# The low parts of the mixer's and the branches' weights on VectorE instead of GpSimd

## The chip, the core and the metric

The kernel runs on one core of a Trainium2 chip. The core has five engines that each work through a queue of their own in order: TensorE (PE in the profile: matmuls, with their weight loads as PEld), VectorE (DVE), ScalarE (ACT), GpSimd (POOL) and SyncE (SP), which here issues most of the loads. The metric is the device time of one execution in microseconds (us), the median over runs. Lower is better.

## The reference, cut to what matters

One layer of a streaming encoder, for 512 tokens of 1024 features in float32:

```python
h = modulate(rmsnorm(x, norm1_g), sh1, sc1)          # sh, sc, gt: columns of silu(c) @ w_ada + b_ada
qa, ka, va, qkb, vb, ob, ib, fb, ga, gb = split(h @ w_in)
y_a = chunk_band_attention(qa, ka, va, rel_bias)     # mixer A, 8 heads x 64
y_b = sigmoid(ob) * rmsnorm(mlstm(silu(conv(qkb)), vb, ib, fb))   # mixer B, 4 heads x 128
y = sigmoid(ga) * (y_a @ w_branch_a) + sigmoid(gb) * (y_b @ w_branch_b)
x = x + gt1 * (y @ w_out)
h2 = modulate(rmsnorm(x, norm2_g), sh2, sc2)
x = x + gt2 * peer_ffn(h2, w_peer_q, peer_sub_keys, peer_u, peer_v)   # 8 heads, best 16 of 128 x 128 experts
out = rmsnorm(x, final_g)
```

## The kernel before

Each large float32 product is made of three matmuls in the type float32r. Both operands are split into a high part (the value rounded to float32r) and a low part (the value minus the high part), and `mm3` (L162 to L165) adds high x high, high x low and low x high in one PSUM bank.

Weights come in pieces of 128 partitions x 1024 numbers, 512 KB each. `load` (L133) lets SP issue the transfer into one of four buffers (`wst`). `split` (L142) then cuts a piece into two halves of 512 columns. For each half ACT copies the high part (`whi`, L150), and one engine subtracts to make the low part (`wlo`, L153). Five buffers of each kind exist. Which engine subtracts is read from a list, `lanes["now"]`, in turn (L151). The list changes with the stage: one list for the start (L897), `LANES_A` (L53) from there to the end of the branches, `LANES_F` for the scores and `LANES_V` for the last stage. The loads of the conditioning weights `w_ada` use the same four `wst` buffers; their dot products are DVE's, at L178.

The stages in order are:

- the start (`start`, L266): the first norm, 16 conditioning columns and the values of both mixers (8 pieces);
- mixer A (`mixer_a`, L317: keys, queries, masked softmax in `ps_s`, `sb` and `mx`) and mixer B (`mixer_b`, L374: gate rows from L389, convolutions in `conv`, L439, head norm from L510), interleaved with each other, with the later conditioning columns (`ada_late`) and with the branch gates (`gates`, L531);
- the branches (`branches`, L545), the output projection and the second norm;
- scores, selection and experts, which take the larger part of the time and start at about 482 us.

The program text gives the order in which work may start, but not the order of each queue: the tile framework plans that from estimated times when the program is built (`schedule_with_timeline_sim=True` in the last lines of the kernel). When the costs or engines of some instructions change, the queues are planned anew.

Of the kernel before, what the change touches and what calls it, by code (L numbers as in the profile page):

```python
# [19 lines left out]
DRAM = bass.MemoryType.DRAM  # L20
# [17 lines left out]
HOLD = 8  # L38
# [4 lines left out]
E1 = 40  # L43
# [8 lines left out]

LANES_A = lambda nc: [nc.gpsimd]  # L53
LANES_F = lambda nc: [nc.vector, nc.gpsimd, nc.gpsimd]
# [6 lines left out]
def weave(*gens):  # L61
    """One generator that steps several in turn; each is (generator, steps per round)."""
    live = [list(g) for g in gens]
    while live:
        for g in list(live):
            for _ in range(g[1]):
                try:
                    next(g[0])
                except StopIteration:
                    live.remove(g)  # L70
                    break
        yield
# [8 lines left out]
def tile_block(  # L81
# [19 lines left out]
    nc = tc.nc  # L101
# [40 lines left out]
    def split(t, pool=None, bufs=WB):  # L142
        """float32 -> two float32r parts whose sum is the value, in two halves."""
        pool = pool or wpool
        parts = []
        for i in range(2):
            cs = slice(i * HW, (i + 1) * HW)
            hi = pool.tile([P, HW], F32R, tag="whi", name="whi", bufs=bufs)
            lo = pool.tile([P, HW], F32R, tag="wlo", name="wlo", bufs=bufs)
            nc.scalar.copy(hi, t[:, cs])  # L150
            e = lanes["now"][rot[0] % len(lanes["now"])]  # L151
            rot[0] += 1
            e.tensor_tensor(out=lo, in0=t[:, cs], in1=hi.bitcast(F32), op=ALU.subtract)  # L153
            parts.append((hi, lo))
        return parts

    def cut(w, a, n):
        """Columns a .. a + n of a split piece."""
        i, o = divmod(a, HW)
        return tuple(x[:, o : o + n] for x in w[i])  # L160
# [10 lines left out]

# [1 line left out]

    def ada(cols):
        """Columns of silu(c) @ w_ada + b_ada."""
        for j in cols:
            t = load(w_ada[j])
            nc.vector.scalar_tensor_tensor(  # L178
                junk(), t, 0.5, state["srow"], op0=ALU.mult, op1=ALU.mult, accum_out=mod[:, j : j + 1]
            )  # L180
        j0, n, step = cols[0], len(cols), cols[1] - cols[0]
        js = slice(j0, j0 + (n - 1) * step + 1, step)
        nc.vector.tensor_add(mod[:, js], mod[:, js], cst[:, C_BADA + js.start : C_BADA + js.stop : step])
# [23 lines left out]
    def rstd_rows(squares):  # L207
        """1 / rms of every token, the same in all partitions, from the squares of blocks of features."""
        ps = bank("w", "ps_ss")
        for i in range(4):  # L210
            for k, sq in enumerate(squares):
                nc.tensor.matmul(
                    ps[:, i : i + 1], sq[:, i * P : (i + 1) * P], ones[:, :1], start=k == 0, stop=k == len(squares) - 1
                )
        rs = spool.tile([P, 4], F32, tag="rs4", name="rs4")
        nc.scalar.activation(rs, ps[:, :4], AF.Sqrt, scale=1.0 / D, bias=epst)
        nc.vector.reciprocal(rs, rs)
        ps = bank("w", "ps_rs")
        for i in range(4):
            nc.tensor.matmul(  # L220
                ps[:, i * P : (i + 1) * P], rs[:, i : i + 1].broadcast_to([P, P]), ident, start=True, stop=True
            )
        return ps

    def norm_block(hT, k, t, rbc, gs, sh0):
        """Modulated RMSNorm of one block of 128 features, split in two parts."""
        h = state["fp"].tile([P, S], F32, tag="hf", name="hf", bufs=3)
        nc.vector.tensor_mul(h, t, rbc)
        nc.scalar.activation(h, h, AF.Identity, scale=gs[:, k : k + 1], bias=mod[:, sh0 + k : sh0 + k + 1])
        nc.scalar.copy(hT[0][:, k, :], h)  # L230
        nc.vector.tensor_sub(hT[1][:, k, :], h, hT[0][:, k, :].bitcast(F32))
        return h
# [4 lines left out]
    pieces = {}  # L237
# [9 lines left out]
    def proj_t(ps, w, hT):  # L247
        """[128 features, tokens]: one piece of 8 x 128 weights."""
        for k in range(KD):
            mm3(ps, cut(w, k * P, P), (hT[0][:, k, :], hT[1][:, k, :]), k == 0, k == KD - 1)  # L250

    def proj_n(ps, nm, j, hT):
        """[tokens, 512 features] for the four token tiles: one of four pieces of 2 x 512 weights."""
        w = piece(nm, j)
        for kk in range(2):
            k = 2 * j + kk
            for i in range(4):
                mm3(
                    ps[i],
                    (hT[0][:, k, i * P : (i + 1) * P], hT[1][:, k, i * P : (i + 1) * P]),  # L260
                    cut(w, kk * 512, 512),
                    k == 0,
                    k == KD - 1,
                )

    def start(ap, bp):  # L266
        """First norm, with the values of both mixers as its blocks come in."""
        hT = features("hT")
# [46 lines left out]

# [1 line left out]
    def mixer_a(ap, hT, va, y_hi, y_lo):  # L317
        """Chunked band attention, heads in pairs."""
        kaT = ap.tile([P, 4, S], F32, name="kaT", bufs=1)
# [54 lines left out]
    def mixer_b(bp, hT, vb, y_hi, y_lo):  # L374
        """mLSTM in its quadratic form, stabilised per row."""
        kbT = bp.tile([P, BH, S], F32, name="kbT", bufs=1)

        # rows of the gates: log input gate, log forget gate, prefix sums per token tile
        wgs = [bp.tile([P, KD, 32 + BH], F32R, name=f"wgs{i}", bufs=1) for i in range(2)]
# [151 lines left out]
    def gates(tp, hT):  # L531
        """tanh(g / 2) of the branch gates, 128 features of both branches at a time."""
        for f in range(KD):
# [11 lines left out]
    def branches(gp, gate, y_hi, y_lo):  # L545
        """Gated sum of the branches, output projection, residual; x2 goes to DRAM."""
        z_hi = gp.tile([P, KD, S], F32R, name="z_hi", bufs=1)
# [57 lines left out]

# [1 line left out]
    def scores(cp, h2T):  # L607
        """Slots (row, column, gate) of the 16 best experts of every token and head."""
        slots = state["slots"]
# [35 lines left out]
    def top16(vals, places, data):  # L645
        """The 16 largest of each row, in order, and where they stand; data is spoilt."""
        nc.vector.max(vals[:, :8], data)
# [5 lines left out]
    def select(cp, h, sv, i16, best, slots):  # L653
        """A head's best 16 sums of one row and one column score, for all tokens."""
        idx = cp.tile([P, 4, 2, TOPK], F32, tag="idx", name="idx")
# [40 lines left out]
    def gathered(cp, i):  # L696
        """A token tile from gathered rows: gelu(u_e . h2) of its slots, then the weighted rows of v."""
        slots = state["slots"][:, i]
# [36 lines left out]
    def build(cp, i, slots):  # L735
        """Gate of every expert for 128 tokens, [column, row, token] blocks, kept in DRAM."""
        ps = bank("g", "ps_slT")
# [36 lines left out]

# [1 line left out]
    def gather_side(cp):  # L776
# [8 lines left out]
    def hidden(e, h2T, tag, g):  # L785
        """gelu(u_e . h2) of 128 experts for the dense token tiles."""
        u = split(load(u_t[e]))
# [4 lines left out]
    def ahead(up, h2T, held):  # L792
        """Hidden values of the first E1 blocks of experts: HOLD of them stay, the others go to DRAM."""
        for e in range(E1):
# [10 lines left out]
    def output(cp, vp, h2T, held):  # L805
        """Sum over all experts of weight x row of v for the dense token tiles."""
        nt = 4 - NG
# [48 lines left out]
    def finish(cp, i, halves):  # L856
        """Residual and final norm of a token tile."""
        if "rows" not in state:
# [25 lines left out]
    def step(g, n):  # L884
        """Steps a generator n times; false when it has ended."""
        return all(next(g, 0) is None for _ in range(n))


    with pool("ypool", 1) as yp, pool("fpool") as fp, ExitStack() as tstack:
# [5 lines left out]
        with pool("bpool") as bp:  # L895
            with pool("apool", side="right") as ap:
                lanes["now"] = [nc.gpsimd, nc.vector]  # L897
                hT, va, vb = start(ap, bp)
# [20 lines left out]
    def paced(main, side, rate):  # L919
        """Steps the side work `rate` times for each step of the main work."""  # L920
        due = 0.0
# [36 lines left out]
def layout(inputs):  # L958
    """The inputs in the order in which the kernel reads them; nothing but copies."""
    f = {k: np.ascontiguousarray(v) for k, v in inputs.items()}  # L960
# [67 lines left out]
```

## Time and profile before

| | |
|---|---|
| runs of the kernel before | 1803.69, 1800.38, 1801.46 us; median 1801.46 |
| span of the profiled execution | 1804.3 us |
| PE, DVE, ACT, POOL busy | 96%, 75%, 47%, 54% of the span |
| start / mixers and gates / branches and output projection | 0 to 62 / 62 to 383 / 383 to 482 us |

The profile records one execution. "Busy" is the time in which an engine executes; waiting and issuing of transfers don't count. A wait is put down to the instruction that ended last before it. In the chain of waits one goes back from the last instruction to what released it, and so on, so an entry there is time on the path that set the end. "issue" in it is time for which the profile shows no reason. [...]

### The profile page before, as it was taken

What the parts mean: (1) busy time and instruction counts of PE and PEld (TensorE: products, weight loads), DVE (VectorE), ACT (ScalarE), POOL (GpSimd) and SP (SyncE); (2) the same over time, 40 slices, a digit from 0 to 9 for tenths busy, and PEclk for the clock granted to TensorE, in tenths of its full rate; (3) what the DMA queues carried; (4) which work ended last, traced back from release to release, by engine and by line L of the source; (5) the groups of instructions that cost most, each with busy time, mean ns of one, the idle gap of its engine ahead of it and who ended that gap; (6) DMA issues with size and microseconds to landing.
All of it is one profiled execution on the core that took longest, in us unless ns stands there. A gap on an engine that the chain in (4) does not pass through costs nothing.

```text
span 1804.3 us, 25525 instructions
## 1 busy us (share of the span) xinstructions
PE 1726.0 (96%) x8671; PEld 1493.6 (83%) x8671; DVE 1353.3 (75%) x2756; ACT 839.1 (47%) x1624; POOL 974.1 (54%) x804
## 2 busy tenths in 40 slices
PE   5999999999999987999989999999999999999997
PEld 4766678878798787888989999999999999998886
DVE  7357655565579998877458888989988998998445
ACT  4534545433543334999734434333443343434443
POOL 1322224444257676887546656766767766673221
PEclk9989999999999998999999999999999999999999
DMA  8423224463232233455798999889999989988552
GB/s 283 151 70 107 95 81 150 164 234 105 107 110 92 88 109 138 190 204 205 266 390 316 326 339 346 324 326 360 324 342 347 349 321 351 346 283 305 209 205 105
DMA packets 129940, 413.35 MB, mean 229 GB/s; under 512 B 12049, under 2 KB 38801, under 8 KB 128274
## 3 DMA queue, kind: packets, MB, share of 16 engines
q1 hardware_dynamic: 91218, 252.33, 39.8%
q0 software_dynamic: 38592, 159.40, 23.4%
q8 instruction: 68, 1.11, 0.2%
q14 instruction: 62, 0.51, 0.1%
HBM read 376.03 MB, written 35.66 MB: 228 GB/s over the span
## 4 chain that ended last, share of the span: by engine, by line
PE 75%; DVE 12%; ACT 6%; DMA 4%; issue 1%; POOL 1%; SPq 0%; DVEq 0%; ACTq 0%; POOLq 0%
PE acc L163 10%; PE acc L165 10%; PE acc L164 10%; PE ps_act L164 8%; PE ps_act L165 8%; PE ps_act L163 8%; ACT gst L767 3%; DMA wst<-in_w_ada 2%; DVE wlo L153 2%; DVE junk L178 1%; PE ps_s L341 1%; PE ps_g L766 1%; ACT oa L761 1%; PE ps_ya L361 1%; PE ps_pq L163 1%
## 5 line engine op out<-in xcount | busy, mean ns | idle before, releaser
L153 POOL TENSOR_TENSOR wlo<-wst,whi 128x512 fp32r<-128x512 f32 x245 | 335.6, 1375 | 374.1 <-ACT whi L150 330.9
L150 ACT CAST whi<-wst 128x512 fp32r<-128x512 f32 x408 | 252.3, 622 | 475.9 <-PE ps_act L164 282.6
L165 PE MATMUL ps_act<-h2T_hi,wlo 128*128 128x384 f32 x1024 | 348.4, 340 | 5.7 <-DVE wlo L153 4.6
L163 PE MATMUL ps_act<-h2T_hi,whi 128*128 128x384 f32 x1024 | 347.4, 339 | 0.0
L164 PE MATMUL ps_act<-h2T_lo,whi 128*128 128x384 f32 x1024 | 347.2, 339 | 0.0
L164 PE MATMUL acc<-wlo,ehi 128*128 128x512 f32 x768 | 299.1, 391 | 0.0
L163 PE MATMUL acc<-whi,ehi 128*128 128x512 f32 x768 | 293.9, 391 | 4.6 <-ACT whi L150 4.6
L165 PE MATMUL acc<-whi,elo 128*128 128x512 f32 x768 | 286.9, 391 | 0.0
L150 ACT CAST whi<-vst 128x512 fp32r<-128x512 f32 x256 | 158.0, 620 | 181.6 <-PE acc L165 144.2
L710 POOL DMA_INDIRECT ur<-in_u_r,ei x128 | 153.7, 1201 | 116.1 <-DVE junk L713 96.0
L153 POOL TENSOR_TENSOR wlo<-vst,whi 128x512 fp32r<-128x512 f32 x85 | 131.7, 1549 | 152.2 <-ACT whi L150 137.1
L724 POOL DMA_INDIRECT vr<-in_v_r,ei x128 | 163.7, 1279 | 89.7 <-DVE sum_v L730 70.4
L165 PEld LDWEIGHTS ps_act<-h2T_hi,wlo 128*128 128x128 f32 x1024 | 194.0, 189 | 8.1 <-DVE wlo L153 5.9
L163 PEld LDWEIGHTS ps_act<-h2T_hi,whi 128*128 128x128 f32 x1024 | 194.3, 190 | 3.7
L164 PEld LDWEIGHTS ps_act<-h2T_lo,whi 128*128 128x128 f32 x1024 | 194.2, 190 | 3.7
L730 DVE SCALAR_TENSOR_TENSOR sum_v<-vr,act,sum_v 128x1024 f32<-128x1024 f32 x127 | 181.2, 1427 | 1.4 <-DMA vr<-in_v_r,ei 0.7
L153 DVE TENSOR_TENSOR wlo<-wst,whi 128x512 fp32r<-128x512 f32 x163 | 132.9, 817 | 60.0 <-ACT whi L150 59.7
L163 PEld LDWEIGHTS acc<-whi,ehi 128*128 128x128 f32 x768 | 144.9, 189 | 33.1 <-ACT whi L150 5.0
L713 DVE SCALAR_TENSOR_TENSOR junk<-ur,h 128x1024 bf16<-128x1024 f32 x128 | 171.0, 1336 | 0.9
L165 PEld LDWEIGHTS acc<-whi,elo 128*128 128x128 f32 x768 | 144.0, 188 | 30.6 <-DVE elo L841 0.4
L164 PEld LDWEIGHTS acc<-wlo,ehi 128*128 128x128 f32 x768 | 144.3, 188 | 28.4
L153 DVE TENSOR_TENSOR wlo<-vst,whi 128x512 fp32r<-128x512 f32 x171 | 132.5, 776 | 28.7 <-ACT whi L150 28.6
(300 smaller groups left out, 3081.0 us busy)
## 6 DMA issues: line engine op xcount, KB each, us to landing
wst<-in_u_t SPq DMA_DIRECT2D x128, 512.0 KB, 5.8
vst<-in_v_e SPq DMA_DIRECT2D x128, 512.0 KB, 6.1
wst<-in_w_pieces SPq DMA_DIRECT2D x76, 512.0 KB, 3.4
wst<-in_w_ada SPq DMA_DIRECT2D x48, 512.0 KB, 4.0
gd<-gst POOLq DMA_DIRECT2D x12, 2048.0 KB, 7.4
gq<-gd SPq DMA_DIRECT2D x16, 1536.0 KB, 15.1
ad<-gelu SPq DMA_DIRECT2D x8, 768.0 KB, 5.5
aq<-ad SPq DMA_DIRECT2D x8, 768.0 KB, 6.0
```

The source lines that it names most:

```text
L150: nc.scalar.copy(hi, t[:, cs])
L153: e.tensor_tensor(out=lo, in0=t[:, cs], in1=hi.bitcast(F32), op=ALU.subtract)
L163: nc.tensor.matmul(o, a[0], b[0], start=first, stop=False)
L164: nc.tensor.matmul(o, a[0], b[1], start=False, stop=False)
L165: return nc.tensor.matmul(o, a[1], b[0], start=False, stop=last)
L178: nc.vector.scalar_tensor_tensor(junk(), t, 0.5, state["srow"], op0=ALU.mult, op1=ALU.mult, accum_out=mod[:, j : j + 1])
L341: nc.tensor.matmul(pss[:, :n], qaT[po : po + 64, cs], kaT[po : po + 64, hp, :n], start=True, stop=True)
L710: nc.gpsimd.indirect_dma_start(out=t, out_offset=None, in_=u_r, in_offset=bass.IndirectOffsetOnAxis(ap=ei[:, j : j + 1], axis=0))
L713: nc.vector.scalar_tensor_tensor(junk(), t, 1.0, state["h2"][i], op0=ALU.mult, op1=ALU.mult, accum_out=act[:, j : j + 1])
L724: nc.gpsimd.indirect_dma_start(out=t, out_offset=None, in_=v_r, in_offset=bass.IndirectOffsetOnAxis(ap=ei[:, j : j + 1], axis=0))
L730: nc.vector.scalar_tensor_tensor(sum_v, t, act[:, j : j + 1], sum_v, op0=ALU.mult, op1=ALU.add)
L767: nc.scalar.copy(st[:, :, t4 * 4 : t4 * 4 + 4].rearrange("p i t -> p t i"), ps.rearrange("p (t i) -> p t i", t=4),)
```

## The change

Two lists of engines are changed. In the start the low parts were made on GpSimd and VectorE by turns and are now all made on VectorE. From there to the end of the branches they were all made on GpSimd and are now all made on VectorE. The lists of the later stages stay. The other lines of the diff take docstrings and comments away and leave the line numbers as they are.

```diff
-LANES_A = lambda nc: [nc.gpsimd]
+LANES_A = lambda nc: [nc.vector]
 LANES_F = lambda nc: [nc.vector, nc.gpsimd, nc.gpsimd]
 LANES_V = lambda nc: [nc.vector, nc.vector, nc.gpsimd]
...
             with pool("apool", side="right") as ap:
-                lanes["now"] = [nc.gpsimd, nc.vector]
+                lanes["now"] = [nc.vector]
                 hT, va, vb = start(ap, bp)
                 lanes["now"] = LANES_A(nc)
```

## Rows read from the trace of the kernel before

**Rows 1.** The page's first part: busy us of each engine, its share of the span, and the number of instructions.

```profile
PE 1726.0 (96%) x8671; PEld 1493.6 (83%) x8671; DVE 1353.3 (75%) x2756; ACT 839.1 (47%) x1624; POOL 974.1 (54%) x804
```

**Rows 2.** Busy time by stage: the stretch in us, its length, the busy us of each engine with the number of instructions, the granted clock of PE, the busy share of the DMA engines and GB/s. The last row sums five stretches from 0 to 482 us.

```profile
105.00:236.00 131.00, 125.06 (x561) 85.87 (x559) 80.86 (x246) 60.88 (x157) 30.57 (x24) 0.93 0.27 89
236.00:383.00 147.00, 143.13 (x651) 112.77 (x650) 80.88 (x166) 66.43 (x156) 55.29 (x44) 0.98 0.46 155
383.00:482.00 99.00, 96.75 (x446) 80.18 (x444) 49.41 (x61) 35.89 (x61) 42.02 (x33) 0.98 0.39 138
sum 482.00, PE 447.92 PEld 343.28 DVE 273.25 ACT 212.63 POOL 158.49; mean PE 89.58 PEld 68.66 DVE 54.65 ACT 42.53 POOL 31.70
```

**Rows 3.** Busy time, columns as in rows 2: PE, PEld, DVE, ACT, POOL, in the score stage.

```profile
540.00:700.00 160.00, 141.55 (x730) 126.23 (x728) 159.42 (x696) 54.13 (x97) 110.83 (x111) 0.97 0.29 100
```

**Rows 4.** What PE waited for from 62 to 482 us: who waited, what for, us in total, times, longest. The longest waits on DVE; further down the list there is no low part of a weight piece (`wlo`).

```profile
PE ps_hbT L524 <- DVE hb L517: 3.9, 1, 3.9
PE ps_s L341 <- DVE mx L346: 2.7, 2, 2.2
...
PE ps_col L429 <- DVE grow L421: 1.7, 1, 1.7
```

**Rows 5.** The chain of waits in the start: start us, us, what.

```profile
21.45 1.62 DVE wlo L153
...
23.91 0.91 issue
...
33.28 1.37 DVE wlo L153
...
49.99 1.58 issue
...
59.55 1.30 POOL wlo L153
```

**Rows 6.** The instructions that write `wlo` from `wst`, over the whole span: how many, shortest, median and longest duration in ns, first and last start in us.

```profile
L153 POOL TENSOR_TENSOR wlo<-wst,whi x245: 1263/1295/2281, 21.0 to 1606.1; 128x512 fp32r<-128x512 f32 x123
...
L153 DVE TENSOR_TENSOR wlo<-wst,whi x163: 664/686/2704, 21.4 to 1598.4; 128x512 fp32r<-128x512 f32 x163
```

**Rows 7.** In the branches: one low part of GpSimd and the DVE instructions beside it from the timeline (start us, us, engine, line, operation), and L559 from the groups of 383 to 482 us (busy us, mean ns of one).

```profile
400.59 1.29 POOL L153 TENSOR_TENSOR wlo<-wst,whi 128x512 fp32r<-128x512 f32 x1 [1.06 <-ACT whi L150]
...
400.07 0.69 DVE L558 SCALAR_TENSOR_TENSOR gb<-gb,ps_br 128x512 f32<-128x512 f32 x1 [1.11 <-PE ps_br L165]
400.80 1.63 DVE L559 TENSOR_TENSOR ga<-ga,gb 128x512 f32<-128x512 f32 x1
...
L559 DVE TENSOR_TENSOR ga<-ga,gb 128x512 f32<-128x512 f32 x8 | 13.0, 1625 | 0.3
```

**Rows 8.** The gate rows of mixer B on DVE: the shortest, median and longest scan in ns, and the scans and the subtraction behind them in the timeline.

```profile
L402 DVE TENSOR_TENSOR_SCAN arow<-ones,mall x4: 386/900/1436, 88.5 to 91.5; 4x128 f32<-4x128 f32 x4
...
88.46 3.41 DVE L402 TENSOR_TENSOR_SCAN arow<-ones,mall 4x128 f32<-4x128 f32 x4
...
91.91 1.58 DVE L403 TENSOR_TENSOR rr<-rr,arow 4x512 f32<-4x512 f32 x1
```

**Rows 9.** Busy time by stretch, columns as in rows 2 (the engines are PE, PEld, DVE, ACT, POOL in that order).

```profile
82.00:94.00 12.00, 10.30 (x47) 8.21 (x46) 6.22 (x13) 8.98 (x12) 5.29 (x4) 1.00 0.15 46
150.00:176.00 26.00, 22.24 (x112) 16.60 (x111) 21.68 (x44) 9.80 (x22) 9.65 (x6) 0.96 0.41 135
323.00:378.00 55.00, 51.13 (x231) 41.13 (x230) 32.00 (x66) 19.15 (x47) 19.78 (x15) 0.98 0.59 201
```

**Rows 10.** DVE's timeline among the convolutions.

```profile
152.00 0.43 DVE L459 TENSOR_SCALAR kbT<-cv 128x512 f32<-128x512 f32 x1
...
157.87 0.74 DVE L451 SCALAR_TENSOR_TENSOR cv<-raw,cst,cv 128x512 f32<-128x512 f32 x1
...
161.00 1.70 DVE L451 SCALAR_TENSOR_TENSOR cv<-raw,cst,cv 128x512 f32<-128x512 f32 x1
...
164.47 1.40 DVE L459 TENSOR_SCALAR kbT<-cv 128x512 f32<-128x512 f32 x1
...
166.36 2.44 DVE L451 SCALAR_TENSOR_TENSOR cv<-raw,cst,cv 128x512 f32<-128x512 f32 x2
...
172.09 1.37 DVE L459 TENSOR_SCALAR kbT<-cv 128x512 f32<-128x512 f32 x1
```

**Rows 11.** The chain of waits ahead of the last head norm.

```profile
330.96 2.20 DVE junk L178 x2
...
336.73 1.23 DVE junk L178 x2
...
338.49 1.72 DVE cv L451
...
343.99 1.63 POOL wlo L153 x2
...
353.44 2.26 DVE junk L178 x2
...
367.09 1.07 issue
```

**Rows 12.** Waits as in rows 4: DVE's from 62 to 383 us, and those of SP's queue of loads from 62 to 480 us.

```profile
DVE junk L178 <- DMA wst<-in_w_ada: 33.9, 21, 4.3
...
SPq L135 <- POOL wlo L153: 211.7, 46, 13.8
```

**Rows 13.** DVE's timeline in the start.

```profile
13.20 0.06 DVE L443 MEMSET raw<- 128x3 f32 x1
```

**Rows 14.** Busy time, columns as in rows 2, in the stretch behind the wait of 3.9 us in rows 4.

```profile
375.50:382.30 6.80, 5.03 (x14) 4.17 (x15) 4.78 (x11) 4.00 (x7) 3.10 (x3) 0.50 0.74 278
```

## The prediction

> **What bounds the kernel now.** I read the engines' totals first, then the busy time by stage, then what TensorE (PE) waits for inside the stages that the change touches, and only then single operations. By the totals PE is busy 96% of the span [rows 1]; the change leaves PE's work alone, so a gain can only be PE idle time that goes away, and a loss PE idle time that appears. The touched work lies in the first 482 us. There VectorE (DVE) is busy 273 us and GpSimd (POOL) 158 us of 482; in the two main mixer stretches DVE is at 62% and 55% [rows 2]. After 482 us nothing is edited. The stretch that follows is DVE's: 159.4 us busy of 160 from 540 to 700 us [rows 3], so a shift at 482 us should be carried to the end rather than absorbed.
>
> From 62 us on the waits of PE name softmax, gate and head-norm results of DVE, 3.9, 2.7 and 1.7 us; a low part of a weight piece (wlo) is not among what it waits for [rows 4]. So from there GpSimd's slow low parts are early enough: making one faster is worth nothing to PE by itself. What can pay is indirect. The last wait for a low part made on GpSimd is in the start, at 59.55 us [rows 5].
>
> **What moves.** The mixers' and branches' 48 pieces (4 ka, 4 qa, 8 qk, 4 ob, 8 ga, 8 gb, 8 br, 8 wo) are split in two halves each: 96 low parts. The start splits 8 pieces, 16 low parts, half of them on GpSimd: 8. So 104 subtractions change engine; no operation, load or matmul is added. One takes 1295 ns (median) on GpSimd and 686 ns on DVE [rows 6]: DVE gets 104 x 0.686 = 71 us more work, GpSimd loses some 135 us.
>
> **What comes back.** A DVE instruction with only SBUF operands stands still while GpSimd subtracts. The clear case is in the branches: GpSimd runs 400.59 to 401.88; DVE's L559 starts at 400.80 and takes 1.63 us, so it ends 0.55 us after GpSimd does; its neighbour of the same size takes 0.69. All eight L559 average 1625 ns [rows 7]. With GpSimd empty those stalls go. So DVE's busy time rises by less than 71 us, and what matters is the balance on the few chains where DVE holds up PE. I price each low part there at 0.69 us and each stalled instruction at its excess over its own undisturbed row.
>
> **Start, 0 to 62 us.** The chain of waits runs load, high part, low part, load. In it a DVE low part takes 1.62 and 1.37 us beside a GpSimd one, and two "issue" waits of 0.91 and 1.58 us lie where DVE stood behind GpSimd; the last link is a GpSimd low part of 1.30 us [rows 5]. On DVE alone a pair takes 2 x 0.69 = 1.38, so the links change by 1.38 - 1.62 = -0.24; about -0.55 for the second pair, whose first half can run while ACT still makes the second high part; 0.69 - 0.91 = -0.22; 0.69 - 1.58 = -0.89; 0.69 - 1.30 = -0.61. Sum -2.5 us. Bounds: -4.7 if none of the added low parts is on the chain (0.93 + 0.68 + 0.91 + 1.58 + 0.61), +1 if DVE's queue makes one more load wait.
>
> **Gate rows, 82 to 94 us.** Here the first PE wait (1.7 us) is made. Four scans take 3.41 us where an undisturbed one takes 0.386 (4 x 0.386 = 1.54), and L403 takes 1.58 against about 0.69 [rows 8]: 1.87 + 0.89 = 2.76 us of stall. GpSimd made four low parts here [rows 9], 4 x 0.69 = 2.76. A wash: 0, between -1.7 (the wait gone) and +2.8.
>
> **Convolutions, 150 to 176 us.** DVE is busy 21.68 of 26 us with six GpSimd low parts beside it [rows 9]. L459 takes 0.43 undisturbed, 1.40 and 1.37 beside them; L451 0.74 against 1.70 and 2.44 for two [rows 10]: excess 0.97 + 0.94 + 0.96 + 0.96 = 3.83. Added 6 x 0.69 = 4.14. Net +0.3, between -2.7 (the wait of PE on the maxima gone [rows 4]) and +4.1.
> [...]
>
> **Head norm, 323 to 378 us.** Here the longest PE wait, 3.9 us, is made [rows 4]. The chain is DVE's dot products for the conditioning (L178) waiting for their loads. On it are stalls again: L178 2.20 and 2.26 against 1.23, L451 1.72 against 0.74, an issue wait of 1.07, and a GpSimd pair of 1.63 that a DVE low part (0.69) would end [rows 11]: 0.97 + 1.03 + 0.98 + 1.07 + 0.94 = 5.0 us. Against it stand up to 15 low parts, 10.4 us. DVE is idle 55 - 32 = 23 us in this stretch [rows 9], for the most part behind L178's loads (33.9 us in 21 waits over the mixer [rows 12]); a low part that falls in such an idle time costs nothing. I take a third of them, 3.3 us, as on the chain: DVE was idle 42% and its queue order decides the rest. Net -1.7, between -5.0 (and with it the half-speed stretch after the wait) and +10.4 - 5.0 = +5.4.
>
> **Branches and output projection, 383 to 482 us.** DVE is busy 49 of 99 us [rows 2] and PE waits for no low part; moving 32 costs 22 us of DVE time and returns 8 x (1.63 - 0.69) = 7.5 us. PE hides all of it: 0. Without that cover, 0.69 us for each.
>
> **Waits that appear.** On GpSimd a low part that waits for its high part holds up nothing. On DVE everything queued behind it waits: softmax maxima, convolution steps, L178. The high part itself waits on ACT for a buffer that PE frees. And SP's loads wait 211.7 us in all for GpSimd's low parts to free their buffers [rows 12]; these waits would be on DVE's queue, which itself stands behind SP's loads at L178. That circle is not in the trace.
>
> **Sum.** -2.5 + 0 + 0.3 - 1.7 + 0 = -3.9 us on the profiled span of 1804.3 us: 1800.4. The runs' median lies 2.8 us below that span (1801.46), so 1797.6; I say 1797.6. [...]
>
> **Rivals.** (1) Forecast, the stalls returned outweigh the low parts added on the chains: 1797.6, chance 0.45. (2) The PE waits are all set by something else (loads, ACT's queue), and PE stays as it is: 1801.5, chance 0.28. For it: the three waits read sum to 8.3 us only [rows 4], and PE is near full. (3) The circle between SP and DVE closes: a low part stands behind L178, the buffer it holds is the next L178's load. Then more than half of the 15 low parts of 323 to 378 us lie on the chain (from 5.0/0.69, about 7, it costs), all of them +5.4; with -2.5 + 0.3 that is +3.2, and with a half-speed stretch behind the longer wait (3.4) +6.6: 1808. Against it: 23 us of DVE idle. Chance 0.21. (4) The 3.9 us wait goes, and the half-speed stretches at it and at 174 us with it: -2.5 - 5.0 - 3.4 - 2.7 = -13.6, 1788, chance 0.06. That the change doesn't do what it says would be (2) with GpSimd still busy before 482 us.
>
> **How the numbers follow.** A measurement of this kernel can tell about 0.2%, 3.6 us, from nothing: below 1797.9 is faster, above 1805.1 slower. Forecast and (4) are faster but the forecast lies at the edge, so some of its chance is "same": faster 0.45, same 0.33, slower 0.22. Range: from 1797.6 - 7.3 - the start's further 2.2, 1788, to (3)'s 1808; 0.2 left out.
>
> **What would show it.** GpSimd nearly idle before 465 us; L559 at 0.6 to 0.7 us, L178 at 1.23; DVE busy about 300 us in the first 482. Right if PE's wait at the head norm shrinks and the score stage begins 3 to 5 us earlier. Wrong if new PE waits for "DVE wlo" appear after 62 us, if DVE's waits for w_ada loads grow past 34 us, or if the end shifts though the first 482 us don't.

## The result, and the profile after

| | before | after |
|---|---|---|
| median of the runs beside each other | 1802.36 us | 1789.55 us |
| ratio, 95% interval | | 0.9931, [0.9911, 0.9950] |
| span of the profiled execution | 1804.3 us | 1787.2 us |

The changed kernel is 0.69% faster, 12.8 us by the medians. A second measurement, among the experiments, gave the same ratio: 0.9931, [0.9913, 0.9949]. The forecast was 1797.6 us, 3.9 us faster, in a range of 1788 to 1808. The side was right and the time lies in the range, near its lower end; the gain is about three times the forecast. The medians of the kernel before differ by a few us from batch to batch (1802 to 1805), so that kernels are compared by their ratios below.

The totals of the page after, to set beside [rows 1], and the busy time up to the first score matmul, to set beside the sum in [rows 2] (PE, PEld, DVE, ACT, POOL, then the granted clock, with 1.00 for full speed, the DMA share and GB/s):

```profile
PE 1711.7 (96%) x8671; PEld 1483.7 (83%) x8671; DVE 1372.9 (77%) x2868; ACT 841.5 (47%) x1624; POOL 824.8 (46%) x692
```

```profile
0.00:465.00 465.00, 437.40 (x1993) 337.52 (x1994) 294.31 (x702) 216.62 (x456) 8.82 (x17) 0.99 0.44 149
```

GpSimd has 112 instructions less and DVE 112 more. The prediction counted 104: there are 52 pieces, not 48, in the mixers and branches (4 + 4 + 8 + 4 + 8 + 8 + 8 + 8), so 104 low parts there and 8 in the start. They are 77 us of work at 0.69 us each; DVE's busy time in the whole first part rose by 21 us only (273.25 to 294.31). The other 56 us are stalls that went away. Single instructions show it. The scans of [rows 8] and L559 of [rows 7] after (ns shortest, median, longest; and busy us, mean ns):

```profile
L402 DVE TENSOR_TENSOR_SCAN arow<-ones,mall x4: 386/387/411, 84.8 to 85.8; 4x128 f32<-4x128 f32 x4
```

```profile
L559 DVE TENSOR_TENSOR ga<-ga,gb 128x512 f32<-128x512 f32 x8 | 5.5, 685 | 0.0
```

What PE waited for from 62 to 482 us after, to set beside [rows 4]:

```profile
PE ps_s L341 <- DVE mx L346: 1.8, 3, 0.8
PE psrow L199 <- DVE diag L198: 1.7, 1, 1.7
PE ps_pt L357 <- DVE sb L354: 1.3, 2, 1.1
PE ps_h L602 <- ACT hf L229: 1.2, 1, 1.2
PE ps_s L341 <- ACT qaT L329: 1.0, 1, 1.0
```

The waits of 3.9 us (`ps_hbT`, the last head norm) and 1.7 us (`ps_col`, the gate rows) are gone; no low part has taken their place. Two short waits just ahead of the scores grew: `ps_h` is new, and `psrow` was 0.7 us before. DVE's and SP's waits, to set beside [rows 12] (DVE from 62 to 365 us, SP from 62 to 465 us):

```profile
DVE wlo L153 <- ACT whi L150: 41.5, 33, 2.7
DVE junk L178 <- DMA wst<-in_w_ada: 18.2, 19, 2.9
```

```profile
SPq L135 <- DVE wlo L153: 185.8, 45, 14.5
```

The new wait is real: DVE now stands 41.5 us for high parts. But its waits for the conditioning loads fell from 33.9 to 18.2 us, and SP waits less for the low parts than before.

**Where the 12 us came from.** Two profiles can't be subtracted blindly. One experiment (the score list alone) has the same PE queue as the kernel before in its first 3015 matmuls, past the start of the scores, and reached the first score matmul at 475.1 us, where the kernel before took 482.0. So I compare stages over all profiled executions, each between the first matmuls into the named tiles, and put side by side the kernels by who makes the low parts in that stage:

| stage (first matmul to first matmul) | low parts on GpSimd, us | low parts on DVE, us | forecast |
|---|---|---|---|
| start, to `ps_ka` | 71.7, 70.0, 70.5 (half of them) | 68.1, 68.5, 69.3, 68.9, 68.3, 68.2, 69.9, 69.6 | -2.5 |
| gate rows, `ps_ka` to `ps_qa` | 31.8, 30.3, 31.7, 31.6 | 28.4, 28.4, 28.4, 28.4, 28.3, 28.4, 28.4 | 0 |
| convolutions, `ps_qa` to `ps_ob` | 115.3, 115.0, 111.3, 111.2 | 109.9, 111.9, 110.4, 110.0, 112.2, 111.8, 112.1 | +0.3 |
| head norms, `ps_ob` to `ps_br` | 164.8, 161.3, 164.7, 162.6 | 158.3, 158.4, 158.3, 158.3, 158.3, 158.4, 158.5 | -1.7 |
| branches, `ps_br` to `ps_pq` | 98.4, 98.5, 98.8, 99.9, 98.9 | 99.9, 100.4, 99.4, 99.8, 99.1, 98.8 | 0 |

The two runs with GpSimd work added are left out here; their stages stand with them below. The differences of the means are -1.9, -3.0, -2.0, -5.0 and +0.7, together -11.2 us, which is within the interval of the ratio (9 to 16 us). Between the two profiles of before's order and the four that keep the changed order to the scores, the start of the scores moves by 478.6 - 465.9 = 12.7 us. The stages that the change leaves alone keep their length: from the first score matmul to the end 1322.3 us before, 1322.6 and 1321.4 after.

**How much of it is the clock.** PE's granted clock falls to 0.50 of its full speed for stretches of 3.4 to 10.3 us. Up to the scores the kernel before has five of them: the one of [rows 14] and these four.

```profile
95.60:99.00 3.40, 3.40 (x8) 2.67 (x9) 2.61 (x7) 1.28 (x3) 1.28 (x1) 0.50 0.01 4
112.70:119.50 6.80, 6.80 (x20) 4.77 (x20) 4.69 (x19) 2.24 (x7) 0.00 (x0) 0.50 0.13 40
174.10:184.40 10.30, 8.93 (x19) 5.25 (x20) 8.68 (x35) 3.30 (x12) 0.00 (x0) 0.50 0.37 127
477.90:482.00 4.10, 3.38 (x17) 3.02 (x15) 2.20 (x5) 2.08 (x4) 0.00 (x0) 0.50 0.22 78
```

The changed kernel's first profile has two, the second shown only up to the first score matmul:

```profile
165.90:172.70 6.80, 5.65 (x15) 4.08 (x15) 4.87 (x21) 2.33 (x8) 0.00 (x0) 0.50 0.44 131
462.90:464.60 1.70, 1.09 (x6) 1.09 (x6) 1.00 (x5) 1.31 (x3) 0.00 (x0) 0.50 0.00 0
```

Each of these seven begins 0.8 to 3.7 us after a wait of PE began, waits of 0.66 to 3.87 us; a wait of 1.02 us in the changed kernel, ahead of its matmul at 103.60 us, has none behind it. What the clock costs shows at the end of the stretch of [rows 14], in the kernel before's chain of waits (start us, us): a matmul of 128x512 takes 0.43 us there and 0.23 us behind it.

```profile
381.35 0.43 PE ps_gb L164
381.77 0.43 PE ps_gb L165
...
383.03 0.23 PE ps_gb L163
383.26 0.23 PE ps_gb L164
```

PE is busy for 27.5 us of the stretches before, and for 18.8 us in the other profile of before's order; for 6.7 and 10.7 us in the two profiles of the changed kernel. By 0.43 against 0.23 about half of that is lost, so the clock accounts for some 7 of the 12.5 us between the two pairs (an estimate). The runs' mean granted clocks agree: 0.985 over 53 runs of the kernel before and 0.989 over 10 of the changed one, which is at most 27 us lost against 20. That leaves 5 to 6 us for the shorter waits and the start.

### The profile page after: what moved, and what is told of

Its sections match the earlier page's. It is cut to its first block, busy times and chain, and to the rows that moved or that the text cites. A ratio compares the mean times of both kernels' runs of the same rounds, so it can differ in the third digit from the quotient of the medians.

```text
span 1787.2 us, 25467 instructions
## 1 busy us (share of the span) xinstructions
PE 1711.7 (96%) x8671; PEld 1483.7 (83%) x8671; DVE 1372.9 (77%) x2868; ACT 841.5 (47%) x1624; POOL 824.8 (46%) x692
## 4 chain that ended last, share of the span: by engine, by line
PE 79%; DVE 9%; ACT 7%; DMA 2%; issue 2%; POOL 1%; SPq 0%; DVEq 0%; ACTq 0%; POOLq 0%
PE acc L165 10%; PE acc L163 10%; PE acc L164 10%; PE ps_act L165 8%; PE ps_act L163 8%; PE ps_act L164 8%; ACT gst L767 4%; DVE wlo L153 1%; ACT oa L761 1%; PE ps_ya L361 1%; PE ps_s L341 1%; PE ps_pq L165 1%; PE ps_pq L163 1%; PE ps_pq L164 1%; PE ps_qk L163 1%
## 5 line engine op out<-in xcount | busy, mean ns | idle before, releaser
L153 DVE TENSOR_TENSOR wlo<-wst,whi 128x512 fp32r<-128x512 f32 x275 | 206.9, 755 | 109.8 <-ACT whi L150 103.8
L153 POOL TENSOR_TENSOR wlo<-wst,whi 128x512 fp32r<-128x512 f32 x133 | 184.6, 1394 | 192.5 <-ACT whi L150 185.8
L164 PEld LDWEIGHTS acc<-wlo,ehi 128*128 128x128 f32 x768 | 144.1, 188 | 28.4
```

What stands on the lines that cost most here:

```text
L164: nc.tensor.matmul(o, a[0], b[1], start=False, stop=False)
```

## The experiments

Three theories were on the table. S: DVE no longer stands still beside GpSimd's reads. L: a low part takes 0.69 us in place of 1.3, so that buffers and loads come earlier. R: the newly planned queue orders happen to be better. Kernels of one batch ran beside their own runs of the kernel before.

**The two edits apart.** The start's list alone:

```diff
-LANES_A = lambda nc: [nc.vector]
+LANES_A = lambda nc: [nc.gpsimd]
```

> Only the start's list is changed; the mixers and branches keep their low parts on GpSimd. Theory S (the gain is DVE no longer standing still beside GpSimd's reads, stage by stage): the start's own 3.5 us, the shift of the last va matmul between the two profiles, so about 0.2% under the kernel before, and the PE wait of 3.9 us ahead of the last head norm is still there. Theory R (the gain is an accident of the newly planned queues): any number within some 8 us of the kernel before, and milestones that move in stages that weren't edited.

Measured: ratio 0.9976, [0.9964, 0.9988]. `LANES_A` alone:

```diff
-                lanes["now"] = [nc.vector]
+                lanes["now"] = [nc.gpsimd, nc.vector]
```

> Only LANES_A is changed; the start keeps its alternation. Theory S: the rest of the gain, some 9 us under the kernel before (0.5%), and the sum of this and the run with the start alone is the whole change's 12.8 us within 3 us. Theory R: the two don't add up.

Measured: 0.9949, [0.9931, 0.9966]. Together -0.24% - 0.51% = -0.75%, against 0.69% for the whole change: they add up. In the first, the gate rows and the head norms take as long as before (31.7 and 164.7 us, table above) and PE's wait ahead of the head norm is there (4.5 us); in the second it is gone. One stage of the first moved without an edit, as R had it: its convolutions are 4 us shorter than in the kernel before; that is taken up below.

**GpSimd's reads put back, the work left on DVE.** In `split`, behind each low part that was moved (`ghost["now"]` is 1 for those, `scr` is scratch):

```diff
+            if ghost["now"][(rot[0] - 1) % len(ghost["now"])]:
+                nc.gpsimd.tensor_tensor(out=scr, in0=hi.bitcast(F32), in1=hi.bitcast(F32), op=ALU.subtract)
```

> The changed kernel, with a subtraction on GpSimd added for every low part that was moved off it: 512 columns, both inputs the high part, the result into scratch that nobody reads. No PE or DVE work differs from the changed kernel. Theory S: DVE stands still beside it again, some 45 us of stalls on top of the 71 us that were moved, so the whole gain goes and the time is at or above the kernel before, 1800 to 1815. Theory L (the gain is that DVE's low part takes 0.69 us where GpSimd's takes 1.3, so that buffers and loads come earlier): the low parts are still DVE's, so most of the gain stays, below 1794. Theory R: anything.

Measured: 0.9986, [0.9972, 1.0001]. The gain is gone within the noise, although every low part is DVE's. L would have kept most of it: a low part takes 0.907 us there, stalls included, still well below GpSimd's 1.295. One side effect comes with the edit: GpSimd also holds the high part's buffer, and ACT waited 12.0 us in 7 waits for that. PE's longest waits, below, are all for results of DVE.

**The same with writes only.** In place of the subtraction, two memsets, the first tied to the high part's copy (`cp`):

```diff
+                ms = nc.gpsimd.memset(scr, 0.0)
+                tc.add_manual_dep(ms.ins, cp.ins.name, mybir.DependencyInfo(mybir.DependencyClass.Sync, mybir.DependencyReason.DATA), reason="paced")
+                nc.gpsimd.memset(scr, 0.0)
```

> As the run with GpSimd's added subtractions, but in their place two memsets of 512 columns into the scratch, each pair waiting for the same high part: GpSimd is as busy at the same times, but writes only. Theory S, with the stall tied to GpSimd's reading: no stalls on DVE, within 3 us of the changed kernel's 1789.6. If any GpSimd work beside DVE stalls it: at or above 1800. Theory R: anything.

Measured: 0.9944, [0.9927, 0.9961]; most of the gain stays, and the interval overlaps the changed kernel's (2.3 us above it by the ratios). The two profiles side by side, subtractions first (line numbers are 2 to 6 higher there). DVE's groups from 0 to 480 us, busy us and mean ns:

```profile
L155 DVE TENSOR_TENSOR wlo<-wst,whi 128x512 fp32r<-128x512 f32 x122 | 109.7, 907 | 33.4 <-ACT whi L152 31.4 <-ACT sb L356 1.0 <-PE ps_qk L168 0.8
L182 DVE SCALAR_TENSOR_TENSOR junk<-wst,srow 128x1024 bf16<-128x1024 f32 x48 | 61.9, 1289 | 24.9 <-DMA wst<-in_w_ada 24.6
```

```profile
L155 DVE TENSOR_TENSOR wlo<-wst,whi 128x512 fp32r<-128x512 f32 x123 | 85.5, 699 | 55.4 <-ACT whi L152 52.2 <-ACT sb L358 2.1 <-PE ps_qk L170 0.8
L184 DVE SCALAR_TENSOR_TENSOR junk<-wst,srow 128x1024 bf16<-128x1024 f32 x48 | 58.7, 1224 | 23.2 <-DMA wst<-in_w_ada 22.9
```

The scans of the gate rows, ns shortest, median and longest:

```profile
L406 DVE TENSOR_TENSOR_SCAN arow<-ones,mall x4: 385/789/1218, 87.2 to 89.8; 4x128 f32<-4x128 f32 x4
```

```profile
L408 DVE TENSOR_TENSOR_SCAN arow<-ones,mall x4: 385/386/414, 85.9 to 86.9; 4x128 f32<-4x128 f32 x4
```

And PE's longest waits from 62 to 480 us with the subtractions:

```profile
PE ps_s L345 <- DVE mx L350: 3.6, 2, 3.1
PE ps_hbT L528 <- DVE hb L521: 3.0, 1, 3.0
```

Beside GpSimd's subtractions (148 us of them) DVE is busy 344 us up to the first score matmul at 480 us; beside its memsets (118 us) 297 up to 469, about as without them (294). With reads the head norm's wait is back at 3.0 us; with writes it isn't in the list. In both runs PE's 8671 matmuls and ACT's 1624 instructions stand in the same order as in the changed kernel, so R, a lucky order, can't be what separates them. Stage by stage as in the table above, reads against writes: 70.5 and 69.1, 29.4 and 28.4, 115.4 and 112.6, 161.6 and 158.3, 103.3 and 101.0 us, together 10.8 us. The added reads start as soon as a high part is there, so they don't meet the same instructions as before: the counterpart of L559 takes 679 ns beside them, and DVE's low parts take about half of the stalls (109.7 against 85.5 us).

So in these two runs it is GpSimd's reading that stalls DVE: DVE's low part, with two inputs in SBUF, takes 907 ns on the mean beside the subtractions, which read SBUF, and 699 beside the memsets, which only write it.

**Where along the kernel.** The branches back on GpSimd:

```diff
         with pool("gpool") as gp:
+            lanes["now"] = [nc.gpsimd]
```

> The changed kernel, with the 32 low parts of the branches and the output projection put back on GpSimd. In the kernel before, L559 took 1.63 us beside them and PE waited for none of it. Theory S with PE as the cover: L559 is back at 1.6 us, DVE is some 14 us less busy there, and the time is the changed kernel's within 2 us (0.7% under the kernel before). If stalls cost wherever they are: 7 us are lost again.

Measured: 0.9927, [0.9905, 0.9949]: L559 takes 1625 ns on the mean again, to the nanosecond as in [rows 7], and no loss shows, since PE waits for none of it; 7 us more would be a ratio of 0.997, outside the interval.

The two halves of the mixer stage:

```diff
-                lanes["now"] = LANES_A(nc)
+                lanes["now"] = [nc.gpsimd]
...
+            lanes["now"] = [nc.vector]
             tp = tstack.enter_context(pool("tpool", KD, side="right"))
```

> Start and everything from the end of mixer A on with low parts on DVE; the interleaved part of the two mixers on GpSimd. Theory S: the start's 3.4 us and the head norm's 6.4 us (the shifts of the changed kernel there) are gained, the 9 us between are not: some 8 to 10 us under the kernel before by the profile, 0.4 to 0.5% by the runs. Theory R: no such pattern; the head norm's gain depends on the queue planned long before it.

Measured: 0.9966, [0.9949, 0.9982]. The reverse, with `[nc.gpsimd]` at the second place only:

> The reverse: start and interleaved part on DVE, everything from the end of mixer A on (gates, last heads, branches) on GpSimd. Theory S: some 12 us earlier until 360 us as in the changed kernel, and then the PE wait ahead of the last head norm is back, 3 to 5 us with a half-speed stretch behind it: about 6 us above the changed kernel, 0.3 to 0.5% under the kernel before. Theory R: no pattern.

Measured: 0.9949, [0.9932, 0.9967]. PE's waits sort themselves by who subtracts at the place: with GpSimd in the interleaved part `ps_col` waits 1.7 us and not with DVE; with GpSimd in the late part `ps_hbT` waits 2.8 us and not with DVE. Late half on DVE first, then early half on DVE:

```profile
PE ps_s L341 <- DVE mx L346: 2.7, 2, 2.2
PE ps_s L341 <- ACT qaT L329: 2.3, 2, 1.3
PE ps_col L429 <- DVE grow L421: 1.7, 1, 1.7
```

```profile
PE ps_hbT L524 <- DVE hb L517: 2.8, 1, 2.8
PE ps_s L341 <- DVE mx L346: 1.8, 3, 0.8
...
PE ps_s L341 <- ACT qaT L329: 1.0, 1, 1.0
```

R is thus not needed for these two waits: in thirteen profiles, with seven different orders of PE's queue up to the scores, they are there where GpSimd reads at the place and nowhere else. The forecast totals of the two runs were right within their intervals, which don't tell the halves apart from each other.

**The score stage, where DVE is full.** All of its low parts on GpSimd:

```diff
-LANES_F = lambda nc: [nc.vector, nc.gpsimd, nc.gpsimd]
+LANES_F = lambda nc: [nc.gpsimd]
```

> The changed kernel, with the score stage's list all GpSimd in place of one DVE and two GpSimd. There DVE is 99% busy, and a low part on it costs 0.68 us and 0.57 us of stall on the mean. Theory S priced by DVE's time: 25 low parts less are 31 us less of DVE's 218 there, some 5 to 8 us of new stalls on selections come back, and the stage ends up to 20 us earlier, as far as PE (190 of 218 us busy) and GpSimd's queue allow: 1775 to 1788. Rival: GpSimd's own selection products (2.5 us each) queue behind the low parts, DVE waits for them, and the time is at or above the changed kernel's.

Measured: 0.9888, [0.9865, 0.9911], 1782.1 us: inside the expected range, and the fastest of all (38 low parts change engine). All of them on DVE (`[nc.vector]`):

> The changed kernel, with all low parts of the score stage on DVE too. Theory S in its two parts, stalls returned and DVE time added: 50 low parts more cost 34 us, of the some 30 us of stalls in that stage the 14 us of the low parts themselves and part of the rest go, since GpSimd's selection products still read beside DVE. DVE is saturated there, so the balance shows in full: 10 to 20 us above the changed kernel, 1798 to 1810. Rival (on DVE is better everywhere, as stalls outweigh the work): at or below 1789.

Measured: 1.0077, [1.0059, 1.0095], 1816.0 us, worse than expected (74 low parts change engine). And the list of the first of these two in the kernel before:

> The kernel before, with the score stage's list all GpSimd and nothing else. If the two edits act on different stages by the same account, this gains what that list gained on top of the changed kernel: 0.4%, some 8 us under the kernel before. If the score stage's gain needs the earlier one: nothing.

Measured: 0.9939, [0.9915, 0.9963], 0.6% where 0.4% was expected; with the 0.69% of the change 1.3%, against the 1.1% that both together gave, the same within the intervals.

> The changed kernel once more beside the last two: 0.69% under the kernel before, within 0.2%.

Measured: 0.9931, [0.9913, 0.9949].

Busy time in the score stage, one third of the low parts on DVE (the changed kernel), none, and all. The rows end 3 to 8 us ahead of the first matmul into `ps_slT`, which follows the selections:

```profile
465.00:680.00 215.00, 197.74 (x1028) 175.35 (x1027) 199.97 (x898) 83.34 (x151) 132.98 (x142) 0.99 0.30 99
```

```profile
466.00:670.00 204.00, 193.32 (x1023) 173.27 (x1022) 183.97 (x875) 84.51 (x154) 161.69 (x165) 0.99 0.32 106
```

```profile
465.00:704.00 239.00, 222.56 (x1154) 200.77 (x1154) 229.57 (x956) 93.58 (x171) 77.63 (x93) 0.97 0.32 106
```

From the first score matmul to the first into `ps_slT` it is 220.2, 207.7 and 246.0 us. The stage follows DVE's busy time: 16 us less work, 12.5 us shorter; 30 us more, 26 us longer (the last row also holds 126 more of PE's matmuls, drawn in from the work that is interleaved with the scores). In the last one GpSimd subtracts no low part, and still DVE's low parts take 914 ns on the mean. GpSimd's selection products of 2.5 us each still read beside them, which fits, though it wasn't tried without them:

```profile
L153 DVE TENSOR_TENSOR wlo<-wst,whi 128x512 fp32r<-128x512 f32 x83 | 75.4, 914 | 7.4 <-PE ps_pq L165 4.6 <-ACT whi L150 2.6 <-issue 0.2
```

So there the move adds the work and returns little: 83 low parts against 24 are 41 us of work at 0.69 us, and DVE is busy 30 us longer, where in the first part 56 of 77 us came back. In this stage, where DVE is busy 93% of the time, low parts are better off on GpSimd: -0.4% one way (0.9888 / 0.9931), +1.5% the other (1.0077 / 0.9931), each within some 0.3%.

## Why the prediction was right, and where it was too small

**The mechanism** was right: stalls of DVE beside GpSimd's subtractions, returned on the chains where DVE holds up PE. The run with reads put back and the one with writes show it, and DVE's busy time fits, 21 us more for 77 us of work. That the stall falls on instructions whose operands are all in SBUF shows in the branches of the kernel before: L559 took 1.63 us [rows 7] where it takes 0.685 after, while L558, which also reads PSUM (`ps_br`), takes 0.68 with a GpSimd subtraction beside it from its start to its end:

```profile
409.12 1.29 POOL L153 TENSOR_TENSOR wlo<-wst,whi 128x512 fp32r<-128x512 f32 x1 [1.80 <-ACT whi L150]
...
409.16 0.68 DVE L558 SCALAR_TENSOR_TENSOR ga<-ga,ps_br 128x512 f32<-128x512 f32 x1
```

The gain is about three times the forecast for two reasons: the sum priced added low parts that PE never felt, and it put the stretches at half clock behind PE's waits at nothing. Those stand only in its range and in rival (4), and they are about half of the gain; without them the forecast of 3.9 us stands against some 5 to 6. The 7.3 us in the range are the longest wait, 3.9 us [rows 4], and half of the 6.8 us at clock 0.50 [rows 14], the same 3.4 us as in rivals (3) and (4): the author's estimate, which no run shows as a term. In its place the runs showed half-clock stretches worth some 7 us, and 5 to 6 us for the shorter waits and the start.

**Start**, -2.5: measured -1.9, with a spread of up to 1.8 us within a column. Right.

**Gate rows**, 0: measured -3.0, and 28.4 us each time with DVE. The step that failed is "4 x 0.69 = 2.76. A wash": it put every added low part on the chain. DVE's timeline after, from the maximum's input to the last step before PE's transposes:

```profile
79.75 0.69 DVE L153 TENSOR_TENSOR wlo<-wst,whi 128x512 fp32r<-128x512 f32 x1 [1.47 <-ACT whi L150]
84.10 0.68 DVE L399 SCALAR_TENSOR_TENSOR mall<-mrow,grow 4x512 f32<-4x512 f32 x1 [3.66 <-ACT grow L398]
84.82 1.36 DVE L402 TENSOR_TENSOR_SCAN arow<-ones,mall 4x128 f32<-4x128 f32 x4
86.11 0.65 DVE L153 TENSOR_TENSOR wlo<-wst,whi 128x512 fp32r<-128x512 f32 x1
...
86.81 0.67 DVE L403 TENSOR_TENSOR rr<-rr,arow 4x512 f32<-4x512 f32 x1
...
87.52 0.62 DVE L421 COPY grow<-rr 4x128 f32<-4x128 f32 x4
```

One low part (86.11) lies on the chain ahead of L421, one (79.75) fell into an idle time, the others come later. The stalls were all on it: 3.41 to 1.36 for the scans and 1.58 to 0.67 for L403. Net -2.96 + 0.65 = -2.3, more than PE's wait of 1.7, which went. The rest is the half-clock stretch behind that wait, which the prediction left out here: three of the profiles with GpSimd have it (3.4 us, at 95.60 before) and take 31.6 to 31.8 us, the fourth has the same wait without it and takes 30.3. So the wait is worth 1.9 us and the stretch 1.4.

**Convolutions**, +0.3: -2.0 in the table, and here the cause is only in part settled. The work between the two matmuls is the same in all runs; what differs is the clock. The stage in the kernel before, in the run with the start alone, in the changed kernel, and in that with reads and with writes added:

```profile
103.50:218.80 115.30, 109.36 (x495) 75.16 (x494) 73.63 (x219) 51.05 (x135) 27.08 (x20) 0.93 0.28 96
```

```profile
99.90:211.20 111.30, 105.50 (x495) 72.60 (x494) 73.39 (x219) 51.08 (x135) 26.70 (x20) 0.97 0.30 99
```

```profile
96.50:206.40 109.90, 104.89 (x495) 72.62 (x494) 75.38 (x238) 51.06 (x134) 0.64 (x1) 0.97 0.31 100
```

```profile
99.90:215.30 115.40, 109.33 (x495) 75.53 (x494) 82.83 (x238) 51.15 (x134) 26.49 (x20) 0.93 0.30 96
```

```profile
97.50:210.10 112.60, 108.06 (x496) 74.64 (x495) 75.94 (x238) 51.07 (x134) 20.77 (x39) 0.94 0.29 97
```

115.3 x 0.93 = 107.2, 111.3 x 0.97 = 108.0, 109.9 x 0.97 = 106.6: in full-speed time (length times granted clock) these three are within 1.4 us. So without the clock the stage moved by some 1 us, near the forecast, and the rest is two half-clock stretches. The later one, at 174 us, lasts 10.3 us before and 6.8 in the changed kernel. The earlier one, at 112.7 us, lasts 6.8 us before; it is missing in one profile of the changed kernel and 3.4 us long in the other, with the same queues, so part of the difference is chance. The run with the start alone has GpSimd's low parts in this stage and the DVE busy time of the kernel before (73.4 against 73.6 us), and still a clock of 0.97; the run with the late half on DVE is like it, at 111.2 us. Reads alone thus don't decide the clock. Yet in the changed kernel's own order they do lengthen the stage: with reads added both stretches are as long as before (6.8 and 10.3 us), with writes 6.8 and 6.8, in the one profile of each. What decides how long PE's clock stays low behind its short waits no run told.

**Head norms**, -1.7: measured -5.0. The stage moved by the very 5.0 us of the summed stalls, but that is in part luck: PE's wait was 2.6 to 4.5 us in the four profiles with GpSimd, and the half-clock stretch behind it 6.8, 3.4, 3.4 and 0 us. The step that failed is "I take a third of them, 3.3 us, as on the chain". None of the low parts made PE wait (there are 14, not 15: [rows 9] counts one other GpSimd instruction): with DVE the stage takes 158.3 to 158.5 us in seven runs, with PE busy for all of it and at full clock, so the whole wait and its half-speed tail went, not a part of them.

```profile
206.40:364.70 158.30, 158.30 (x726) 123.64 (x726) 98.38 (x237) 77.85 (x181) 2.84 (x3) 1.00 0.44 150
```

DVE's idle time in its waits for loads took the low parts, as the prediction's bound of -5.0 had it for this stage, and those waits themselves shrank.

**Branches**, 0: +0.7. The run that put them back on GpSimd took 98.9 us there, within what the others take (98.4 to 100.4), so the cover by PE holds. The changed kernel's own two profiles (99.9 and 100.4 us) hold the longer `ps_h` and `psrow` waits (1.2, and 1.7 or 1.8 us), which name no low part.

**Waits that appear**, rival (3): the circle between SP and DVE didn't close. SP's wait for low parts fell from 211.7 to 185.8 us and DVE's for conditioning loads nearly halved.

**Carried to the end**: yes, within 1 us (1322.3 against 1322.6 and 1321.4; 1320.4 to 1327.5 in the other runs with the same score list).

Of the cases on record rival (4), at 1788 with a chance of 0.06, came nearest to the measured time. It had the wait at the head norm and the half-speed stretch behind it go as a whole, which they did. Its other half was luck: the stretch at 174 us got 3.5 us shorter but didn't go, and the earlier one in the same stage, which it didn't name, went or got shorter instead. What was mis-sized is the price of an added low part on a chain: a third to all of 0.69 us in the prediction, next to nothing in the runs as long as DVE had idle time at the place; and the half-clock stretches, nothing in the sum, were worth some 7 us.

## What to carry to other kernels

Before giving elementwise work to an idle GpSimd, look in DVE's timeline for instructions of the same shape at two durations (here 1.63 and 0.685 us for L559); where the long ones run beside a GpSimd instruction that reads SBUF, as they did here, the "free" engine is charged to DVE. Price a move in both directions, stalls returned and time added, stage by stage: a stall lies on whatever chain it hits, while an added instruction off the chain slips into idle time if there is any, and delays the stage if there is none (74 of them cost 26 us in the score stage). Count what follows a wait of PE too: at the gate rows the stretch at half clock behind it was worth 1.4 us, beside 1.9 us for the wait. Compare stages over several profiled executions, with the granted clock beside them, before a single difference of a few us is explained.

## What the runs showed of the hardware that was not expected

Small instructions were stalled too: scans of 4 x 128 that take 0.386 us alone took up to 1.436 beside GpSimd's subtractions [rows 8]. A GpSimd that only writes, 118 us of memsets in the first 470 us, left the same scans at 0.386, with memsets running beside them from 85.8 to 88.1 us. And the same queue order, run twice, reached the same matmul 6.9 us apart within 480 us; in the changed kernel a stretch at half clock lasted 3.4 us in one execution and was missing in the other.
